# Layer 0's squares summed on TensorE, the plain products of the seven moved in front, and the last output projection by seven products too

## The chip, the cores and the metric

One NeuronCore of one Trainium2 chip runs the whole kernel in one launch. The metric is the device time of that launch in microseconds (us), the median of several runs. Where a sum is made against one profiled execution, that execution's own time and span are used.

## The reference, cut to what matters

A decoder trunk of two layers on 512 tokens of 1024 channels, all in float32. In each layer:

```
hdn = rms_norm(x, norm_w)                     # x: 512 x 1024
u   = hdn @ w_in                              # w_in: 1024 x 10240
q,k,v,z of branch A; q,k,v,z of branch B; gates ga, gb = split(u)
ya  = dilated_mixture(qa, ka, va) * silu(za)  # 16 heads of 64
yb  = rms_norm(diff_attention(qb, kb, vb)) * silu(zb)   # 8 heads of 128
merged = sigmoid(ga) * (ya @ w_proj_a) + sigmoid(gb) * (yb @ w_proj_b)
x   = x + merged @ w_out
```

and after both layers `out = rms_norm(x, final_norm_w)`. A rotation of part of q and k by tables of cosines and sines, the causal masks and the scalar lambda of the second branch do not bear on this change.

## The kernel before, in words

**Operands.** Activations lie with the channels on the partitions: eight blocks m of 128 channels x 512 tokens. Every float32 operand of a large product is split in two fp32r parts, a rounded one (`hi`, a ScalarE copy) and the rest (`lo`, a VectorE subtraction), and a product is three matmuls: hi.hi, hi.lo, lo.hi. `h_block` (L186) makes the two parts of one block of x times norm_w; the factor 1/rms of each token is applied later, to the results.

**Weights** come in the order in which `plan` (L917) lists them, in pieces of 128 x 1024 that `load_to` loads on SyncE's queue (L96), and `split` makes `whi` on ScalarE (L102) and `wlo` on VectorE (L103), into pools of three buffers each. `prep_to(i)` is called from the steps of a projection and keeps this two pieces ahead.

**Two ways to project.** `proj_T` (L270) takes 256 output channels by 512 tokens: 16 steps of three 128x512 matmuls into a PSUM tile `pj` of pool `psj` (three buffers). The first one of a layer (`first=True`, the silu gate z0) goes block by block over k, into two tiles of pool `pss` (tag "s"), and calls `rstd_cols` and `layer_tables` at its end. `proj_V` (L307) is for the last output projection alone: 256 channels at a time, four times, for each of four token blocks eight steps of three 128x256 matmuls, into `pv`. `proj_S` (L329) is for v: tokens and contraction are halved, the 1024 output channels come in two halves, and the product is made of seven quarter products in place of eight, in a scheme after Strassen and Winograd. Product i is 8 steps (kk = 0 to 3, a = 0, 1) of three 128x512 matmuls. Products 0, 3 and 6 take plain blocks of h; 1, 2, 4 and 5 take sums S1 to S4 of h's quarters, which `h_sums` makes on VectorE (L221 to L227) and `h_split` splits (L234, L235). The weight quarters 11, 21, 22 are plain; T1 = 12 - 11 and T3 = 12 - 22 are made by `sum_of` (L108): a ScalarE copy times -1 (L111), then a DMA of the POOL queue that adds 12 to it from memory (L112); T2 = T1 - 22 and the last "21" + T2 are VectorE's (L134, L136). Products go to X (pool `pss`, two buffers), Y (`psj`) and Z (pool `pst`, two buffers); `keep` copies a partial result on ScalarE (L349), `add` joins two on VectorE (L353).

**The front.** For layer 0 the blocks of x arrive by DMA (L801, L804). ScalarE makes each block's h (L188), its squares (`sq_block`, L202) and later x times norm_w in place (`h_full`, L197); VectorE the lo part (L189). GpSimd adds the first seven squares one to the other (L206). `rstd_cols` (L242) sums over channels by eight float32 matmuls with a column of ones (L248): two tiles of squares by four token blocks; VectorE adds the two halves (L250, L251), GpSimd raises to the power -1/2 (L240). `rstd_rows` and `layer_tables` spread the result over the partitions (`rb`), and `ev_z` multiplies a gate's PSUM tile by it (L461). Layer 1 does the same with blocks that layer 0's output projection makes one by one.

**The order** within a layer: z0, z1, v of branch A, one q-k projection, v of branch B, then all other projections with the attention heads merged between them, then `pb` (four projections of yb) and the output projection. A scheduler orders each engine's queue by data and program order, and gives out the buffers; the pool `blk` has 29 buffers of 4 KB a partition, which hold h, the operand parts, the raw quarters of weights, y, the gates, `mg` (the merged operand) and, at the end, `xo` (residual, four) and `fwb` (final norm weight, one).

**The end.** `pb`'s evacuation (L716 to L725) makes a block of merged (L720, L721) and splits it to `mg` (L724, L725). `final_out` (L764) adds each 128 x 256 result to the residual (L770), takes squares with a running sum (L772, ScalarE), multiplies by the final norm's weight (L778); after the fourth piece of a token block come the sum and factor (L775 to L777), two scalings (L780 on ScalarE, L782 on VectorE) and two output DMAs (L781, L783).

Of the kernel before, what the change touches and what calls it, by code (L numbers as in the profile page):

```python
# [16 lines left out]
P = 128  # L17
# [6 lines left out]
BIG = 1e30  # L24
SWAP = [(i ^ 8) if i < 16 else i for i in range(32)]
# [7 lines left out]
def trunk_kernel(ctx: ExitStack, tc: tile.TileContext, x, ws, norm_w, subln_w, final_w, lams, negb, rope, ident_in,  # L33
# [148 lines left out]
    st_ = {"y": {}, "z": {}, "v": {}, "qk": {}}  # L182
# [16 lines left out]
    def sq_block(m, xt):  # L199
# [3 lines left out]
        if m == 0:  # L203
# [38 lines left out]
    def rstd_cols():  # L242

        ps = pst.tile([P, T], F32, tag="t", name="ps_ss")
        for n, sq in enumerate((st_["acc"], st_["sq7"])):
            for tb in range(4):
                c = 4 * n + tb
                nc.tensor.matmul(ps[:, c:c + 1], sq[:, tb * P:(tb + 1) * P], ones[:, 0:1], start=True, stop=True)  # L248
        r = small.tile([P, 4], F32, tag="rstd", name="rstd", bufs=2)
        nc.vector.tensor_copy(r, ps[:, 0:4])  # L250
        nc.vector.tensor_tensor(r, r, ps[:, 4:8], OP.add)  # L251
        inv_sqrt(r, r, 1.0 / D, 1e-6)
# [15 lines left out]
    def proj_T(what, rhs, evac, first=False):  # L268
# [38 lines left out]
    def proj_V(what, lhs, evac):  # L307

        steps = []
        c, j0 = next_chunk(what)  # L310
        hold = {}

        def step(tb, k):
            if tb == 0 and k == 0:
                prep_to(j0 + 2)
            if k == 0:
                hold[tb] = psj.tile([P, T], F32, tag="pj", name=f"pv{c}_{tb}")
            hb, t = lhs(k), slice(tb * P, tb * P + P)
            tok3(hold[tb][:, :256], hb[:, 0, t], hb[:, 1, t], j0 + k // 4, 256 * (k % 4), 256, k == 0, k == 7)
            if tb == 3 and k == 3:  # L320
                prep_to(j0 + 3)
            if k == 7:
                evac(tb, hold.pop(tb))
        for tb in range(4):
            for k in range(8):
                steps.append((360, lambda tb=tb, k=k: step(tb, k)))
        return steps

    def proj_S(what, evac, hook=None):  # L329
# [385 lines left out]
    def pb(layer, i):  # L715

        def ev(b, ps):
# [93 lines left out]
    with tc.manual_schedule(engines={mybir.EngineType.Activation, mybir.EngineType.DVE}):  # L811
        for m in range(NB):
# [8 lines left out]
            if m > 1:  # L821
                sq_block(m - 2, xs[m // 2 - 1][:, m % 2])
# [187 lines left out]
```

## Time and profile before

| | us |
|---|---|
| median of 3 runs | 1391.7 |
| lowest, highest | 1388.79, 1391.72 |
| the profiled execution | 1392.57 |
| its span in the trace | 1390.8 |

The trace gives every instruction's start and length on TensorE (PE; its weight loads PEld), VectorE (DVE), ScalarE (ACT), GpSimd (POOL) and SyncE (SP; a q behind an engine's name is its queue). Times are from the start of the span. Matmuls are pipelined: a 128x512 matmul has a length of 0.39 us, and the next one starts before it ends. PEclk is the granted TensorE clock as a share of 2.4 GHz.

### The profile page before, as it was taken

Reading aid. Unit: us, or ns where it says so; the run is one execution under the profiler, and the core shown is the slowest. Engines: PE = TensorE matmul, PEld = TensorE weight load, DVE = VectorE, ACT = ScalarE, POOL = GpSimd, SP = SyncE. Lnnn points to the kernel's source line nnn. Section 1 sums busy time; section 2 is a strip of 40 time slices with the busy share of each in tenths; the row PEclk is TensorE's granted clock in tenths of the full one; section 3 lists DMA queues with packets and bytes.
Section 4 is the critical chain, followed back from the end, with each engine's and each line's share of the span. In section 5 each row is a group of like instructions: output and inputs, shape, how many; then the busy total and the mean of one; then the engine's idle time right before and its main releaser. Section 6 shows DMA issues by size and latency. Waiting matters only on the chain.

```text
span 1390.8 us, 19560 instructions
## 1 busy us (share of the span) xinstructions
PE 1356.6 (98%) x6728; PEld 1138.8 (82%) x6728; DVE 971.6 (70%) x1900; ACT 859.2 (62%) x1630; POOL 335.7 (24%) x459
## 2 busy tenths in 40 slices
PE   7999999999999999999999999999999999999996
PEld 5788887878888888888878888877888888888896
DVE  6766887779767786545576777797796678664553
ACT  8655678877565757523566566778756566664332
POOL 4120342334303241110220224232350133211000
PEclk9999999999999999999999999999999999999998
DMA  9663574546735564433686366554565364535321
GB/s 305 172 165 123 131 188 102 164 129 158 177 121 144 136 175 116 127 107 91 201 252 150 96 177 159 145 139 121 145 171 163 110 186 114 152 95 162 115 91 61
DMA packets 82019, 202.95 MB, mean 146 GB/s; under 512 B 11136, under 2 KB 27648, under 8 KB 81920
## 3 DMA queue, kind: packets, MB, share of 16 engines
q1 hardware_dynamic: 45312, 134.57, 31.0%
q0 software_dynamic: 19712, 58.74, 18.8%
q10 hardware_dynamic: 16896, 8.39, 2.1%
q8 instruction: 53, 0.87, 0.3%
q14 instruction: 46, 0.38, 0.1%
HBM read 134.55 MB, written 16.78 MB: 109 GB/s over the span
## 4 chain that ended last, share of the span: by engine, by line
PE 91%; DVE 3%; DMA 2%; ACT 1%; issue 1%; POOL 1%; SPq 0%; POOLq 0%; DVEq 0%; ACTq 0%
PE pj L282 21%; PE pj L283 21%; PE pj L284 21%; PE X L304 2%; PE X L305 2%; PE X L303 2%; PE Y L304 1%; PE Y L305 1%; PE Y L303 1%; PE pv L303 1%; PE pv L305 1%; PE pv L304 1%; DMA T<-ws_d 1%; DMA kx(1, 0, 2)0_7658<-hl(1, 0, 2)1_7655 1%; DVE wlo L103 1%
## 5 line engine op out<-in xcount | busy, mean ns | idle before, releaser
L282 PE MATMUL pj<-h,whi 128*128 128x512 f32 x1024 | 405.4, 397 | 7.6 <-DVE whi L817 6.5
L283 PE MATMUL pj<-h,whi 128*128 128x512 f32 x1024 | 407.0, 397 | 1.2 <-DVE h L189 1.1
L284 PE MATMUL pj<-h,wlo 128*128 128x512 f32 x1024 | 403.5, 396 | 0.0
L103 DVE TENSOR_TENSOR wlo<-raw,whi 128x1024 fp32r<-128x1024 f32 x207 | 264.8, 1280 | 103.8 <-ACT whi L102 103.3
L102 ACT ACTIVATE whi<-raw 128x1024 fp32r<-128x1024 f32 x207 | 219.0, 1059 | 148.1 <-PE pj L283 95.5
L282 PEld LDWEIGHTS pj<-h,whi 128*128 128x128 f32 x1024 | 193.4, 189 | 47.0 <-issue 6.5
L283 PEld LDWEIGHTS pj<-h,whi 128*128 128x128 f32 x1024 | 193.6, 189 | 39.3 <-DVE h L189 2.9
L284 PEld LDWEIGHTS pj<-h,wlo 128*128 128x128 f32 x1024 | 193.6, 189 | 37.1 <-DVE wlo L103 0.3
L712 POOL TENSOR_TENSOR g<-g,pr 128x512 f32<-128x512 f32 x16 | 21.0, 1313 | 151.4 <-ACT g L711 126.4
L206 POOL TENSOR_TENSOR sq<-sq,sq 128x512 f32<-128x512 f32 x12 | 19.7, 1642 | 88.1 <-ACT sq L202 87.7
L103 DVE TENSOR_TENSOR wlo<-T,whi 128x1024 fp32r<-128x1024 f32 x24 | 29.3, 1224 | 15.2 <-ACT whi L102 15.1
L304 PE MATMUL pv<-wlo,mg 128*128 128x256 f32 x128 | 35.7, 283 | 0.0
L305 PE MATMUL pv<-whi,mg 128*128 128x256 f32 x128 | 35.7, 283 | 0.0
L303 PE MATMUL pv<-whi,mg 128*128 128x256 f32 x128 | 35.4, 283 | 0.0
L720 DVE TENSOR_TENSOR g<-pj,g 128x512 f32<-128x512 f32 x16 | 11.1, 692 | 30.5 <-PE pj L284 30.5
L102 ACT ACTIVATE whi<-T 128x1024 fp32r<-128x1024 f32 x24 | 25.2, 1056 | 10.8 <-DVE T L134 3.9
L709 DVE TENSOR_TENSOR g<-pj,rb 128x512 f32<-128x512 f32 x32 | 21.4, 686 | 10.8 <-PE pj L284 10.6
L724 ACT ACTIVATE mg<-g 128x512 fp32r<-128x512 f32 x16 | 10.1, 632 | 29.5 <-DVE g L721 29.5
L112 POOL DMA_DIRECT2D T<-ws_d x16 | 14.6, 930 | 53.9 <-ACT T L111 43.3
L303 PE MATMUL X<-whi,h 128*128 128x512 f32 x64 | 23.9, 402 | 3.7 <-DVE z(0, 0, 0)_292 L461 2.5
L496 ACT ACT_TABLE_LOAD x21 | 26.9, 1283 | 0.4
L304 PE MATMUL X<-wlo,h 128*128 128x512 f32 x64 | 25.8, 403 | 0.4 <-DVE wlo L103 0.4
(4000 smaller groups left out, 3307.6 us busy)
## 6 DMA issues: line engine op xcount, KB each, us to landing
raw<-ws_d SPq DMA_DIRECT2D x199, 512.0 KB, 3.9
T<-ws_d POOLq DMA_DIRECT2D x16, 512.0 KB, 7.8
v_dram<-c ACTq DMA_DIRECT2D x24, 256.0 KB, 2.6
pa_dram<-pa SPq DMA_DIRECT2D x16, 256.0 KB, 3.0
pr<-pa_dram SPq DMA_DIRECT2D x16, 256.0 KB, 4.1
v_dram<-v ACTq DMA_DIRECT2D x8, 256.0 KB, 5.9
xr<-x_d SPq DMA_DIRECT2D x8, 256.0 KB, 4.5
x_dram<-xr SPq DMA_DIRECT2D x8, 256.0 KB, 2.7
```

Of the source, the lines that this page charges most:

```text
L102: nc.scalar.activation(whi[j], src, AF.Copy)
L103: nc.vector.tensor_tensor(wlo[j], src, bits(whi[j]), OP.subtract)
L206: nc.gpsimd.tensor_tensor(st_["acc"], st_["acc"], s, OP.add)
L282: nc.tensor.matmul(ps, w_h, hb[:, 0], start=(k == 0), stop=False)
L283: nc.tensor.matmul(ps, w_h, hb[:, 1], start=False, stop=False)
L284: nc.tensor.matmul(ps, w_l, hb[:, 0], start=False, stop=(k == 7))
L303: nc.tensor.matmul(ps, hh, w_h, start=first, stop=False, skip_group_check=True)
L304: nc.tensor.matmul(ps, hh, w_l, start=False, stop=False, skip_group_check=True)
L305: nc.tensor.matmul(ps, hl, w_h, start=False, stop=last, skip_group_check=True)
L496: nc.scalar.activation(p, p, AF.Exp, bias=mn[:, i:i + 1], scale=-1.0, accum_out=den[:, i:i + 1])
L709: nc.vector.tensor_tensor(g[:, b], ps, rb, OP.mult)
L712: nc.gpsimd.tensor_tensor(g[:, 0], g[:, 0], st_.pop(("pa", m)), OP.mult)
```

## The change

Three parts. **First**, layer 0's squares are no longer added on GpSimd: `sq_block` sums each block over its channels at once by four float32 matmuls with the column of ones, into one PSUM tile of pool `pst` that is cleared first and read by `inv_sqrt` directly. x times norm_w for layer 0 is made by VectorE in place of ScalarE. Layer 1 keeps GpSimd's additions. **Second**, the seven products run in the order 0, 3, 1, 2, 4, 5, 6, the two that need plain h and plain weights first; loads, weight splits and sums are reordered to match, the first tile of z0 goes to pool `pso` and its second to `psj`, so that X's pool `pss` is free, and product 6 runs a = 0 before a = 1. S3 and S4 are computed together with S1 and S2. **Third**, the last output projection is made by `proj_S` in place of `proj_V`: merged is kept in float32 too (`mf`, four buffers of `blk`), S1 to S4 are made of it, and the evacuation works on 128 x 512.

```diff
+ORDER = (0, 3, 1, 2, 4, 5, 6)
...
-            need += [n + k for k in (3, 4, 4, 4, 5, 6, 6, 6)] + [n + 8] * 6
+            need += [n + 3, n + 4, n + 5, n + 6] + [n + 6] * 4 + [n + 8] * 6
...
-        if i < 2:
-            q[c, "22", p] = raw.pop(l0 + 2 + p)
-        elif i in (6, 7):
-            q[c, "21", p] = raw.pop(l0 + 4 + p)
-        name = ("11", "T1", "T2", "21", "T3", "22", "21")[i // 2]
+        if i in (2, 3):
+            q[c, "21", p] = raw.pop(l0 + 2 + p)
+            q[c, "22", p] = raw.pop(l0 + 4 + p)
+        name = ("11", "21", "T1", "T2", "T3", "22", "21")[i // 2]
         split(j, flat(q[c, name, p]))
-        if i < 2:
+        if i in (2, 3):
             sum_of(c, "T3", p, q[c, "22", p], ws[l0 + 6 + p])
-        elif i < 4:
+        elif i in (4, 5):
...
-    def sq_block(m, xt):
+    def sq_block(layer, m, xt):
         s = t2(f"sq{m}")
         nc.scalar.activation(s, xt, AF.Square)
-        if m == 0:
+        if layer == 0:
+            if m == 0:
+                st_["ps_ss"] = pst.tile([P, T], F32, tag="t", name="ps_s0")
+                nc.vector.memset(st_["ps_ss"][:, 0:4], 0.0)
+            for tb in range(4):
+                nc.tensor.matmul(st_["ps_ss"][:, tb:tb + 1], s[:, tb * P:(tb + 1) * P], ones[:, 0:1], start=False,
+                                 stop=(m == 7), skip_group_check=True)
+        elif m == 0:
             st_["acc"] = s
...
+        if "ps_ss" in st_:
+            inv_sqrt(r, st_.pop("ps_ss"), 1.0 / D, 1e-6)
+        else:
...
-                pool, tag = (pss, "s") if first else (psj, "pj")
+                pool, tag = (pso, "o") if first and b == 0 else (psj, "pj")
...
-        for i in range(7):
-            for kk in range(4):
-                for a in range(2):
-                    steps.append((683, lambda i=i, kk=kk, a=a: step(i, kk, a)))
+        for i in ORDER:
+            for kk, a in [(kk, a) for kk in range(4) for a in range(2)] if i != 6 else [(kk, a) for a in range(2) for kk in range(4)]:
+                steps.append((683, lambda i=i, kk=kk, a=a: step(i, kk, a)))
...
-            nc.vector.tensor_tensor(g[:, 0], g[:, 0], g[:, 1], OP.add)
+            f = g[:, 0]
+            if layer + 1 == DEPTH:
+                hf = st_["hf"].setdefault(DEPTH, {})
+                if b == 0:
+                    hf[i] = f4(f"mf{i}")
+                f = hf[i][:, b]
+            nc.vector.tensor_tensor(f, g[:, 0], g[:, 1], OP.add)
...
-    def final_out(i):
+    def final_out():
+        seen = set()
-        def ev(tb, ps):
+        def ev(tb, n, src):
+            r = xo[tb][:, n]
+            nc.vector.tensor_tensor(r, src, r, OP.add)
+            scr = t2(f"scr{n}{tb}")
+            nc.scalar.activation(scr, r, AF.Square, accum_out=ssq[:, tb, n:n + 1])
+            both = tb in seen
+            seen.add(tb)
+            if both:
                 rs = small.tile([P, 2], F32, tag="rf", name=f"rf{tb}")
-                nc.vector.tensor_reduce(rs[:, 0:1], ssq[:, tb], mybir.AxisListType.X, OP.add)
+                nc.vector.tensor_tensor(rs[:, 0:1], ssq[:, tb, 0:1], ssq[:, tb, 1:2], OP.add)
...
-            nc.vector.tensor_tensor(r, r, f, OP.mult)
+            nc.vector.tensor_tensor(r, r, fwb[:, n], OP.mult)
...
-        return lambda: proj_V((DEPTH - 1, "out", i), lambda k: st_["mg", k], ev)
+        return proj_S((DEPTH - 1, "out"), ev)
...
     for m in range(NB):
-        h_full(0, m, xs[m // 2][:, m % 2])
+        xt = xs[m // 2][:, m % 2]
+        nc.vector.tensor_scalar(xt, xt, nw[:, 0, m:m + 1], None, OP.mult)
...
-            run(chain(*[final_out(i) for i in range(4)]))
+            f = final_out()
+            h_sums(DEPTH, ("S1", "S2"))
+            h_split(DEPTH, ("S1", "S2"))
+            h_sums(DEPTH, ("S3", "S4"))
+            run(f[:12] + [(0, lambda: h_split(DEPTH, ("S3", "S4")))] + f[12:])
```

## Rows read from the trace of the kernel before

**Rows 1.** The page's first two parts: busy time of TensorE over the span, and the mean busy share of the 16 DMA engines in 40 slices of the span (tenths).
```profile
PE 1356.6 (98%) x6728; PEld 1138.8 (82%) x6728; DVE 971.6 (70%) x1900; ACT 859.2 (62%) x1630; POOL 335.7 (24%) x459
...
DMA  9663574546735564433686366554565364535321
```

**Rows 2.** Busy time by stretch (us from the span's start): length, then busy time and count of PE, PEld, DVE, ACT, POOL, then granted clock, DMA share, GB/s.
```profile
38.00:46.00 8.00, 5.51 (x16) 4.16 (x17) 8.00 (x16) 2.68 (x3) 0.00 (x0) 0.79 1.02 303
41.90:45.40 3.50, 3.50 (x10) 2.71 (x9) 3.50 (x8) 0.73 (x1) 0.00 (x0) 0.51 1.03 335
46.00:84.00 38.00, 38.00 (x170) 31.43 (x169) 25.28 (x32) 27.31 (x34) 2.63 (x3) 1.00 0.54 129
287.70:291.10 3.40, 3.40 (x9) 2.47 (x10) 3.40 (x10) 0.75 (x4) 2.56 (x2) 0.50 0.74 239
...
1311.00:1333.00 22.00, 22.00 (x106) 18.18 (x105) 11.75 (x15) 8.01 (x12) 0.00 (x0) 1.00 0.26 89
1346.00:1380.00 34.00, 33.98 (x284) 33.77 (x282) 16.25 (x38) 11.81 (x31) 1.64 (x3) 1.00 0.19 63
```

**Rows 3.** What PE waited for in the first 60 us, after the first load: us in total, times, longest.
```profile
PE X L303 <- DVE z(0, 0, 0)_292 L461: 2.5, 1, 2.5
PE ps_ss L248 <- POOL sq L206: 1.2, 1, 1.2
...
PE Y L303 <- ACT whi L102: 0.9, 1, 0.9
```

**Rows 4.** The timeline of layer 0's front on PE: start, length, engine, line, operation, count, and the idle time before it.
```profile
14.04 0.39 PE L284 MATMUL pj<-h,wlo 128*128 128x512 f32 x1
...
24.43 1.95 PE L248 MATMUL ps_ss<-ones,sq 128*128 128x1 f32 x16 [1.22 <-POOL sq L206]
26.24 0.48 PE L284 MATMUL pj<-h,wlo 128*128 128x512 f32 x1
...
36.69 0.39 PE L284 MATMUL pj<-h,wlo 128*128 128x512 f32 x1
...
40.99 0.50 PE L303 MATMUL X<-whi,h 128*128 128x512 f32 x1 [2.49 <-DVE z(0, 0, 0)_292 L461]
...
48.17 0.39 PE L303 MATMUL Y<-whi,S 128*128 128x512 f32 x1
```

**Rows 5.** The timeline on PE where layer 1 passes from z1 to v.
```profile
717.85 0.39 PE L284 MATMUL pj<-h,wlo 128*128 128x512 f32 x1
719.47 0.50 PE L303 MATMUL X<-whi,h 128*128 128x512 f32 x1 [1.23 <-DVE z(1, 0, 0)_6533 L461]
...
723.37 0.50 PE L304 MATMUL X<-wlo,h 128*128 128x512 f32 x1 [0.40 <-DVE wlo L103]
```

**Rows 6.** The chain of work that ended last, in v's stage of layer 0: start, length, what. The rows are the first matmuls of two products that follow one another.
```profile
58.99 0.45 PE Z L303 x2
...
64.43 0.45 PE X L303 x2
```

**Rows 7.** The timeline of the last output projection: its first and last matmul on PE, then the last token block's evacuation on DVE, ACT, DVE and ACT.
```profile
1333.74 0.28 PE L303 MATMUL pv<-whi,mg 128*128 128x256 f32 x1
...
1379.70 0.28 PE L305 MATMUL pv<-whi,mg 128*128 128x256 f32 x1
...
1380.01 0.42 DVE L770 TENSOR_TENSOR xo<-pv,xo 128x256 f32<-128x256 f32 x1
...
1380.53 0.42 ACT L772 ACTIVATE scr<-xo 128x256 f32<-128x256 f32 x1 [0.37 <-DVE xo L770]
...
1381.15 0.41 DVE L778 TENSOR_TENSOR xo<-xo,fwb 128x256 f32<-128x256 f32 x1
...
1382.29 0.72 ACT L780 ACTIVATE xo<-xo,rf 128x512 f32<-128x512 f32 x1 [1.24 <-POOL rf L777]
```

**Rows 8.** The timeline of layer 0's front on DVE, POOL and ACT; the second and third row merge four and six instructions.
```profile
10.31 0.75 DVE L189 SCALAR_TENSOR_TENSOR h<-x,nw,h 128x512 fp32r<-128x512 f32 x1 [1.10 <-ACT h L188]
...
14.15 6.88 DVE L189 SCALAR_TENSOR_TENSOR h<-x,nw,h 128x512 fp32r<-128x512 f32 x4
...
13.57 10.81 POOL L206 TENSOR_TENSOR sq<-sq,sq 128x512 f32<-128x512 f32 x6 [12.52 <-ACT sq L202]
...
18.04 1.66 ACT L202 ACTIVATE sq<-x 128x512 f32<-128x512 f32 x3
```

**Rows 9.** DVE's groups by line and shape: busy time, mean ns of one, idle time before. Then, from DVE's timeline, instructions that follow one another without a gap, in pairs or single.
```profile
L721 DVE TENSOR_TENSOR g<-g 128x512 f32<-128x512 f32 x16 | 11.1, 693 | 0.8
...
L782 DVE TENSOR_SCALAR xo<-xo,rf 128x512 f32<-128x512 f32 x4 | 1.9, 488 | 2.3 <-POOL rf L777 2.3
...
28.57 1.28 DVE L225 TENSOR_TENSOR S3f<-x 128x512 f32<-128x512 f32 x2
29.77 1.29 DVE L227 TENSOR_TENSOR S4f<-x,S2f 128x512 f32<-128x512 f32 x2
...
57.14 1.22 DVE L136 TENSOR_TENSOR raw<-raw,T 128x1024 f32<-128x1024 f32 x1
58.28 1.22 DVE L103 TENSOR_TENSOR wlo<-raw,whi 128x1024 fp32r<-128x1024 f32 x1
```

**Rows 10.** DMA issues of the weights: size of one, median us from issue to landing.
```profile
raw<-ws_d SPq DMA_DIRECT2D x199, 512.0 KB, 3.9
T<-ws_d POOLq DMA_DIRECT2D x16, 512.0 KB, 7.8
```

More of the change, by code (lines that the diff above doesn't have):

```diff
@@ L180, in trunk_kernel @@
     nc.gpsimd.memset(bits(pt1[:, :, 0:128]), 0.0)
-    st_ = {"y": {}, "z": {}, "v": {}, "qk": {}}
+    st_ = {"y": {}, "z": {}, "qk": {}, "mg": {}}
     def h_block(layer, m, xt):
@@ L242, in rstd_cols @@
     def rstd_cols():
[L244 to L248, printed above, removed]
-        r = small.tile([P, 4], F32, tag="rstd", name="rstd", bufs=2)
-        nc.vector.tensor_copy(r, ps[:, 0:4])
-        nc.vector.tensor_tensor(r, r, ps[:, 4:8], OP.add)
-        inv_sqrt(r, r, 1.0 / D, 1e-6)
+        r = small.tile([P, 4], F32, tag="rstd", name="rstd", bufs=2)
+        if "ps_ss" in st_:
+            inv_sqrt(r, st_.pop("ps_ss"), 1.0 / D, 1e-6)
+        else:
+            ps = pst.tile([P, T], F32, tag="t", name="ps_ss")
+            for n, sq in enumerate((st_["acc"], st_["sq7"])):
+                for tb in range(4):
+                    c = 4 * n + tb
+                    nc.tensor.matmul(ps[:, c:c + 1], sq[:, tb * P:(tb + 1) * P], ones[:, 0:1], start=True, stop=True)
+            nc.vector.tensor_copy(r, ps[:, 0:4])
+            nc.vector.tensor_tensor(r, r, ps[:, 4:8], OP.add)
+            inv_sqrt(r, r, 1.0 / D, 1e-6)
         st_["rcol"] = r
@@ L305, in tok3, with proj_S @@
         nc.tensor.matmul(ps, hl, w_h, start=False, stop=last, skip_group_check=True)
[L307 to L329, printed above, removed]
+    def proj_S(what, evac):
         steps = []
@@ L335, in proj_S @@
         X, Y, Z, cp = {}, {}, {}, {}
+        plain = st_["mg"] if what[1] == "out" else st_["h"]
         def operand(i, kk, a):
             if i in (0, 3, 6):
-                hb = st_["h"][kk + (0, 4)[i > 0]]
+                hb = plain[kk + (0, 4)[i > 0]]
                 o = 128 * a + (256 if i == 6 else 0)
@@ L372, in step @@
         def step(i, kk, a):
-            if a == 0 and kk % 2 == 0:
-                prep_to(j0 + 2 * i + kk // 2 + 2)
+            if kk % 2 == 0:
+                prep_to(j0 + 2 * ORDER.index(i) + kk // 2 + 2)
             if kk == 0:
@@ L741, in ev @@
             nc.sync.dma_start(x1_dram[layer, m], r)
-            sq_block(m, r)
+            sq_block(layer + 1, m, r)
             h_full(layer + 1, m, r)
-        return lambda: [(0, pre)] + proj_T((layer, "out", i), lambda k: st_["mg", k], ev)
+        return lambda: [(0, pre)] + proj_T((layer, "out", i), lambda k: st_["mg"][k], ev)
     xo = {}
@@ L858, in trunk_kernel @@
         z0, z1 = zz(layer, 0, 0, True)(), zz(layer, 0, 1)()
-        run(z0 + z1[:4] + [(0, lambda: h_sums(layer, ("S1", "S2"))), (0, lambda: h_split(layer, ("S1", "S2")))] + z1[4:])
+        run(z0 + z1[:4] + [(0, lambda: h_sums(layer, ("S1", "S2"))), (0, lambda: h_split(layer, ("S1", "S2"))),
+                           (0, lambda: h_sums(layer, ("S3", "S4")))] + z1[4:])
+        v = vs(layer, 0)()
+        run(v[:12] + [(0, lambda: h_split(layer, ("S3", "S4")))] + v[12:])
         if layer == 0:
             lambdas()
-        v = vs(layer, 0)()
-        run(v[:4] + [(0, lambda: h_sums(layer, ("S3", "S4")))] + v[4:12] + [(0, lambda: h_split(layer, ("S3", "S4")))] + v[12:])
         run(qk(layer, 0, 0)())
@@ L884, in trunk_kernel @@
             nc.sync.dma_start(fwb, bass.AP(tensor=final_w.tensor, offset=final_w.offset, ap=[[0, P], [1, D]]))
-            ssq = small.tile([P, 4, 4], F32, tag="ssq", name="ssq", bufs=1)
+            ssq = small.tile([P, 4, 2], F32, tag="ssq", name="ssq", bufs=1)
             run(chain(*[pb(layer, i) for i in range(4)]), residual_cols(0) + residual_cols(1))
-            run(chain(*[final_out(i) for i in range(4)]))
+            f = final_out()
[3 more added lines that the diff above has]
+            run(f[:12] + [(0, lambda: h_split(DEPTH, ("S3", "S4")))] + f[12:])
         else:
@@ L924, in plan @@
         order = [("z", 0, 0), ("z", 0, 1), ("v", 0), ("qk", 0, 0), ("v", 1)] + [n for p in PARTS for n in p[0]]
-        order += [(n, i) for n in ("pb", "out") for i in range(4)]
+        order += [("pb", i) for i in range(4)] + ([("out", i) for i in range(4)] if layer + 1 < DEPTH else [("out",)])
         for n in order:
-            kind = "S" if n[0] == "v" else "T"
+            kind = "S" if n[0] == "v" or n == ("out",) else "T"
             chunks.append((kind, (layer, *n)))
```

29 lines of the change are left out of this document (10 added, 19 removed).

## The prediction

> **What bounds the kernel now.** I read the page's busy times first: TensorE is busy 98% of the span, so time is won only by taking matmul time out or by filling holes between matmuls [rows 1]. Next the stretches. In the whole stage of seven products PE has no hole (38.00 of 38.00 us) and DVE is busy 25 of 38; in the last output projection PE has none either (33.98 of 34.00) while DVE is busy 16 of 34; the hole lies at 38 to 46, PE 5.5 us busy of 8 [rows 2]. The waits name it: X's first matmul waits 2.5 us for z0's evacuation, because z0 holds pool `pss`; 0.9 us go to a weight half, 1.2 us to GpSimd's sum of squares [rows 3]. Behind it the clock is granted at 0.51 from 41.9 to 45.4, its 1.2 GHz level: that is 1.7 us of work lost, after PE had run one matmul between 36.9 and 41.0 [rows 2, 3, 4]. Layer 1 has the same wait, 1.23 us, and one of 0.40 [rows 5].
>
> **The price of a matmul.** Two products of v start 5.44 us apart [rows 6]; that is 24 matmuls of 512 columns, 0.227 us each. The last projection's 384 matmuls of 256 columns run from 1333.74 to 1379.70 [rows 7]: 45.96 / 383 = 0.120 us each. So a column costs 0.000443 us in the wide ones and 0.00047 in the narrow.
>
> **Part 1, the front of layer 0.** Eight square tiles x 4 matmuls with ones make 64 instructions on PE where 16 stood (each call appears as two): 16 took 24.43 to 26.24, 0.113 us each [rows 4], so 64 cost 7.2 us, 5.4 more. They stay on PE's path, since PE is behind its data from here on. In return GpSimd's six additions (10.8 us) go. While they run, DVE's lo parts take 1.7 us each (four in 6.88), against 0.75 before [rows 8], and PE waits for them: so h's last four blocks come by ScalarE's pace. ScalarE also sheds the eight copies of `h_full`; DVE gets eight tensor_scalars, 0.49 each by the nearest row (L782) [rows 9], 3.9 us. I put these at nothing: z1's eleven us of matmuls cover them; without cover they would cost 3.9.
> New path: at 14.27 PE has done blocks 0 to 3 of z0 [rows 4]. What is left until product 0 is done: 24 matmuls of z0, 48 of z1, 24 of product 0, 96 x 0.227 = 21.8; squares 7.2; the four transposes for rb 0.5. If it never waits it ends at 43.8. The last squares are out at 19.7 even now [rows 8], when PE still has 3 us of z0 queued. Before, product 0 ended at 48.17, with one stray matmul of Y in it: 47.9. Gain 4.1.
> No wait for z0 is left: product 0 goes to X in `pss`, now free, product 3 to Z in `pst`; Y, which needs a `psj` buffer of z0 or z1, starts 10.9 us later. No hole, so no fall of the clock, I take.
> Bounds: the squares' matmuls can each hold up PE's in-order queue for ScalarE, and if the clock falls once that is another 1.7 us; that gives 1.0. If GpSimd's release lets h come still earlier, and weight loads hide under matmuls, 5.5.
> The Trainium skill (TensorE: Matmul & The Clock Gate, Back-to-back issue gap) gives a matmul of up to 64 columns about 25 ns. By that figure the squares would cost an estimated 1.6 us and this part's gain be 9.7. The trace has 113 ns, with a 128*128 weight tile for each, and decides.
>
> **Part 2, the new order elsewhere.** In layer 1 the two holes go: 1.23 + 0.40 = 1.6 us. Bounds 0 (another wait takes their place) and 2. After product 0 PE never waited in layer 0 (46 to 84 us) [rows 2]; I take the other stages of v to be alike, so there the order changes nothing. T1 moves from third to fifth place among the splits, which slackens its adding DMA (7.8 us to land against 3.9 for a plain load) [rows 10]; weight quarter 21 is needed 5.4 us after the start in place of 16. Its load is 3.9 us and is issued ahead: nothing, unless `blk` has no buffer (below). Queues: T3's two adds leave POOL later, and GpSimd's queue is emptier than before.
>
> **Part 3, the last projection.** PE: 7 x 5.44 = 38.1 us in place of 46.1: 8.0 less. But DVE, half idle there, gets the sums. Counted from the stage's start to PE's last matmul: 13 lo parts of weights, 2 T2 and 2 sums "21"+T2, 17 of 128x1024; three operations of the last `mg`; 4 sums S that need the last blocks (the other 4 fit into the idle 10 of 22 us of `pb` [rows 2]); 6 of 8 lo parts of S; 6 joins; 7 residual adds and 7 norm products: 33 of 128x512; 3 scalings. One behind the other, 128x1024 takes 1.14 us (57.14 to 58.28), 128x512 0.60 (two in 1.20) [rows 9]. Sum 19.4 + 19.8 + 1.5 = **40.7 us**, above PE's 38.1. With each at its full length, 1.22 and 0.69, it is 45.0. So the end is no longer TensorE's alone.
> I measure to the last block's scaling, at 1382.29, 48.55 us after the start [rows 7]; what follows (two DMAs and the end) stays. PE bound: 38.1, then the present 2.47 from the last matmul to the scaling, and 0.75 for a block twice as wide (add 0.42 to 0.69, square 0.42 to some 0.62, as three in 1.66, product 0.41 to 0.69 [rows 7, 8, 9]): 41.3, a gain of 7.2. DVE bound: 40.7, then of the last block's 3.2 us (2.47 + 0.75) what queued work cannot fill: its add and product, 1.2, and two waits on ScalarE and GpSimd, an estimated 0.55 each; 43.0, a gain of 5.5. At full lengths 47.3, a gain of 1.2. I take 43.0, since the count is nearer to back-to-back. DVE's lag delays first the residual adds and norm products, which nobody waits for until the end; if the scheduler puts them ahead of weight parts, PE waits in their place, and the sum is the same.
> Buffers: at the start of the stage `blk` holds 8 y (freed one by one in the last 5 us of `pb`), 8 mg, 4 mf, 4 xo, fwb, 2 quarters 11, 2 T1: 29 of 29. Quarters 21 and 22 get the y's places 5 us ahead, and land 3.9 us later. So I put buffers at nothing, with no room to spare.
> The Trainium skill (same page and section) puts the spacing at N/2.4 + 2.5 ns, 216 and 109 ns here. By it PE's part would shrink from 41.9 to 36.3, by 5.6 and not 8.0. This trace has 227 and 120, and decides.
>
> **Sum.** 4.1 + 1.6 + 5.5 = 11.2 us from the profiled execution's 1392.6: 1381.4. That execution stands 0.9 above the median of the runs, so against the median it is 1380.5. I say **1381**.
>
> **The rivals.**
> *The last stage gives little.* DVE's work at full lengths, or PE waiting for lo parts behind evacuations, leaves 1.2 us: 1392.6 - 4.1 - 1.6 - 1.2 - 0.9 = 1384.8 against the median. For it: 40.7 against 38.1 has no slack. Against: much of it can slide past PE's end. 0.2.
> *The front's gain is not there.* The wait for z0 was only the last of several: the DMA engines' share is 1.02 from 38 to 46 us [rows 2], so quarter 21, now wanted at 44, could come late, or the squares' 5.4 us eat the rest. Then part 1 gives 0 and the time is 1392.6 - 1.6 - 5.5 - 0.9 = 1384.6. For it: that share. Against: quarter 21's competitors, 22 and T3, move behind it. 0.13.
> *Slower: `blk` runs dry in the last stage.* If 21 and 22 get buffers only as mg's first four go, 5.4 us into the stage, then product 3 waits for load (3.9) and split (2.2): 6 us, and a clock fall of 1.7. The same at T3 and T2, three times in all: 23 us, against 5.5 + 5.7 gained: 1380.5 + 23 = 1403. It decides when more than 11 us are lost, that is from the second such wait on. For it: the count of 29. Against: y's eight places come free before. 0.05.
> *The change does not do what it says*, the scheduler ordering PE as before: 1391 to 1392. 0.04.
>
> **How the numbers follow.** Forecast 0.58; rivals 0.2, 0.13, 0.05, 0.04. The ends of the three terms, 1.0 + 0 + 1.2 and 5.5 + 2 + 7.2, give 1389.5 and 1377.0 against the median; a clock fall as at 287.7 [rows 2], 1.7 us, may come or go with the shift. All lowest ends at once is unlikely; both middle rivals lie near 1385, with 1.7 us for a clock fall near 1387; one more fall less than today takes the low end to 1375.5. Range **1375.5 to 1387**. Over 0.2% (2.8 us, about what a measurement of this kernel can tell from no change) faster: forecast, two middle rivals, less a share where two of these meet, 0.87; within 0.06; slower 0.07.
>
> **What would show each step.** Front: product 0's last matmul at about 44, PE's idle time before X gone, 64 ps_ss instructions of 0.11 us, DVE's lo parts at 0.75 with no GpSimd additions beside them, clock 1.0 from 42 to 45. Layer 1: no wait between z1 and X. End: from the first X matmul to PE's last 38 to 40 us, DVE busy over 90% in that stretch, the last scaling 43 us after the start. I am wrong if PE waits in the last stage for DMA or for VectorE by more than 3 us, if product 0 still ends past 47, or if holes arise in branch A's v stage.

## The result, and the profile after

The changed kernel takes 1404.82 us (median of 6 runs, 1402.84 to 1407.73) where the kernel before takes 1391.71 (6 runs, 1388.79 to 1392.28): 1.0103 of the time, 95% interval 1.0091 to 1.0114. The forecast was 1381, a gain of 11 us; it became a loss of 13. The profiled execution is the fastest of the six, 1402.84 us with a span of 1401.1.

The page first (it answers to [rows 1]): matmul records went from 6728 to 6560, and TensorE's busy time rose all the same, by 6 us.

```profile
PE 1362.8 (97%) x6560; PEld 1137.4 (81%) x6560; DVE 992.1 (71%) x1923; ACT 867.0 (62%) x1630; POOL 329.8 (24%) x457
...
DMA  9636574545735454332576456554565373535431
...
raw<-ws_d SPq DMA_DIRECT2D x197, 512.0 KB, 3.8
T<-ws_d POOLq DMA_DIRECT2D x20, 512.0 KB, 7.5
```

Busy time by stretch, columns as in [rows 2]. The hole at 38 to 46 is gone, as forecast. In its place stands a stretch of 13.65 us at half clock, in which PE is busy from end to end. Half clock comes four times more, for 3.4 us each; the last row is the last projection from its first matmul to its last:

```profile
14.81:28.46 13.65, 13.65 (x59) 12.97 (x59) 13.10 (x26) 9.19 (x14) 2.99 (x3) 0.51 1.05 369
38.00:46.00 8.00, 8.00 (x37) 6.62 (x36) 5.69 (x6) 3.44 (x4) 3.13 (x2) 1.00 0.59 143
46.00:84.00 38.00, 37.99 (x168) 31.14 (x167) 23.21 (x22) 24.84 (x31) 1.74 (x2) 1.00 0.50 127
294.80:298.20 3.40, 3.40 (x9) 2.62 (x9) 3.40 (x10) 1.97 (x6) 1.88 (x2) 0.51 0.44 171
799.90:803.30 3.40, 3.40 (x10) 2.60 (x9) 1.22 (x1) 0.61 (x1) 0.00 (x0) 0.52 0.02 7
977.50:980.90 3.40, 3.40 (x10) 2.65 (x9) 3.25 (x7) 2.09 (x6) 1.64 (x2) 0.50 0.61 202
1363.20:1366.60 3.40, 3.40 (x10) 2.63 (x9) 3.40 (x5) 0.72 (x2) 0.00 (x0) 0.50 0.00 0
1343.20:1388.20 45.00, 40.66 (x169) 32.26 (x167) 41.84 (x59) 26.58 (x42) 3.25 (x4) 0.96 0.13 24
```

PE's timeline in the front (compare [rows 4]). 56 of the 64 one-column matmuls stand in one block ahead of z0's later blocks. X follows z1 with no wait, and product 0's last matmul starts at 50.25:

```profile
12.76 0.95 PE L208 MATMUL ps_s<-ones,sq 128*128 128x1 f32 x8
...
14.12 11.18 PE L208 MATMUL ps_s<-ones,sq 128*128 128x1 f32 x56
25.16 0.77 PE L292 MATMUL pj<-h,whi 128*128 128x512 f32 x1
...
44.81 0.39 PE L294 MATMUL pj<-h,wlo 128*128 128x512 f32 x1
45.03 0.39 PE L313 MATMUL X<-whi,h 128*128 128x512 f32 x1
...
50.25 0.39 PE L315 MATMUL X<-whi,h 128*128 128x512 f32 x1
```

What PE waited for, in three stretches (0 to 130, 690 to 810, 1335 to 1395; us in total, times, longest). The waits of [rows 3, 5] for z0's evacuation and for GpSimd's squares are gone. Three new kinds have come: 2.0 us in each stage of branch B's v, 1.5 us behind layer 1's z1, 4.3 us in the last stage:

```profile
PE X L313 <- ACT c L338: 2.0, 1, 2.0
...
PE X L313 <- ACT c L338: 2.0, 1, 2.0
PE X L314 <- DVE wlo L104: 1.5, 1, 1.5
...
PE Y L314 <- DVE wlo L104: 4.3, 2, 2.9
```

The last stage's first and last matmul and its last scalings (compare [rows 7]): 44.7 us of matmuls where 46.0 were, and 3.75 us from the last matmul to the last scaling where 2.59 were.

```profile
1343.21 0.39 PE L313 MATMUL X<-whi,mg 128*128 128x512 f32 x1
...
1387.93 0.39 PE L315 MATMUL X<-whi,mg 128*128 128x512 f32 x1
...
1391.68 1.04 DVE L777 TENSOR_SCALAR xo<-xo,rf 128x512 f32<-128x512 f32 x2 [0.37 <-POOL rf L772]
1391.68 1.33 ACT L775 ACTIVATE xo<-xo,rf 128x512 f32<-128x512 f32 x2 [1.35 <-POOL rf L772]
```

**Where the 10.3 us between the two profiled spans (1390.8 and 1401.1) arose**, by PE's milestones: branch A's v of layer 0 ends 2.8 us later; branch B's v adds 2.3; the rest of layer 0 adds 0.9; layer 1's front and branch A's v give 0.1 back (the wait for z0 is gone, one for a lo part has come); layer 1's branch B and the way to the last stage add 3.5; the last stage gives 1.2 back; the tail behind PE's last matmul takes 2.1 more.

Counted by the clock, the kernel before has three stretches of half clock while PE works, the two of [rows 2] and this one:

```profile
966.90:970.30 3.40, 3.24 (x8) 2.46 (x9) 3.40 (x10) 0.99 (x5) 2.26 (x2) 0.50 0.89 236
```

Each costs 1.7 us of work, 5.1 together; in the changed kernel one of 13.65 and four of 3.4 us cost 13.6. So some 8.5 of the 10.3 us are lost at half clock: 5.1 more in the front, 1.7 each behind the waits that end at 799 and 1362. Such a stretch comes or goes with the execution: near 285 to 295 PE waits some 2 us in all in every kernel traced, and half clock follows in the kernel before and the changed one but not in e6, e8, e9 and e10 below. A difference of 1.7 us between two profiled executions therefore proves little by itself.

### The profile page after: what moved, and what is told of

Read it like the earlier page. It is cut to its first block, busy times and chain, and to the rows that moved or that the text cites. A ratio compares the mean times of both kernels' runs of the same rounds, so it can differ in the third digit from the quotient of the medians.

```text
span 1401.1 us, 19220 instructions
## 1 busy us (share of the span) xinstructions
PE 1362.8 (97%) x6560; PEld 1137.4 (81%) x6560; DVE 992.1 (71%) x1923; ACT 867.0 (62%) x1630; POOL 329.8 (24%) x457
## 4 chain that ended last, share of the span: by engine, by line
PE 88%; DVE 5%; DMA 3%; ACT 1%; issue 1%; POOL 1%; SPq 0%; ACTq 0%; DVEq 0%; POOLq 0%
PE pj L292 21%; PE pj L293 21%; PE pj L294 21%; PE X L313 2%; PE X L314 2%; PE X L315 2%; DMA T<-ws_d 1%; DVE wlo L104 1%; DMA raw<-ws_d 1%; PE Y L314 1%; PE Y L315 1%; PE ps_s L208 1%; PE Y L313 1%; DVE S L242 0%; DMA x<-x_d 0%
## 5 line engine op out<-in xcount | busy, mean ns | idle before, releaser
L104 DVE TENSOR_TENSOR wlo<-T,whi 128x1024 fp32r<-128x1024 f32 x30 | 36.6, 1221 | 21.5 <-ACT whi L103 21.5
L113 POOL DMA_DIRECT2D T<-ws_d x20 | 18.1, 949 | 129.6 <-ACT T L112 114.9
L103 ACT ACTIVATE whi<-T 128x1024 fp32r<-128x1024 f32 x30 | 31.7, 1056 | 16.9 <-DMA T<-ws_d 8.3
L314 PE MATMUL Y<-wlo,S 128*128 128x512 f32 x80 | 32.0, 399 | 4.3 <-DVE wlo L104 4.3
L313 PE MATMUL X<-whi,S 128*128 128x512 f32 x80 | 30.7, 404 | 4.0 <-ACT c L338 4.0
L314 PE MATMUL X<-wlo,S 128*128 128x512 f32 x80 | 32.0, 400 | 0.0
L315 PE MATMUL Y<-whi,S 128*128 128x512 f32 x80 | 31.9, 398 | 0.0
L315 PE MATMUL X<-whi,S 128*128 128x512 f32 x80 | 31.8, 397 | 0.0
L112 ACT ACTIVATE T<-raw 128x1024 f32<-128x1024 f32 x20 | 20.5, 1052 | 15.2 <-DMA raw<-ws_d 10.9
L313 PE MATMUL Y<-whi,S 128*128 128x512 f32 x80 | 28.4, 395 | 0.0
```

Source lines behind the costliest of these rows:

```text
L103: nc.scalar.activation(whi[j], src, AF.Copy)
L104: nc.vector.tensor_tensor(wlo[j], src, bits(whi[j]), OP.subtract)
L112: nc.scalar.activation(flat(t), flat(of), AF.Copy, scale=-1.0)
L313: nc.tensor.matmul(ps, hh, w_h, start=first, stop=False, skip_group_check=True)
L314: nc.tensor.matmul(ps, hh, w_l, start=False, stop=False, skip_group_check=True)
L315: nc.tensor.matmul(ps, hl, w_h, start=False, stop=last, skip_group_check=True)
```

## The experiments

Twelve kernels ran. Ratios are to the kernel before, run on the same chip in the same session. A name stands for the kernel from here on. The kernel before measured 1390.75 to 1391.71 in these sessions, so medians of two sessions compare to about 1 us.

| kernel | squares of layer 0 | T3 | last projection | median us | ratio (95%) |
|---|---|---|---|---|---|
| changed | TensorE, in a block | late | seven products | 1404.82 | 1.0103 (1.0091 to 1.0114) |
| e1 | GpSimd | late | seven products | 1399.99 | 1.0072 (1.0058 to 1.0085) |
| e2 | TensorE, in a block | early | seven products | 1392.60 | 1.0014 (1.0006 to 1.0023) |
| e3 | TensorE, in a block | late | as before | 1400.14 | 1.0066 (1.0052 to 1.0079) |
| e4 | TensorE, spread | late | seven products | 1399.10 | 1.0064 (1.0050 to 1.0077) |
| e5 | TensorE, in a block | early | no lo parts | 1387.10 | 0.9972 (0.9961 to 0.9983) |
| e6 | TensorE, spread | early | as before | 1387.92 | 0.9976 (0.9966 to 0.9986) |
| e7 | TensorE, spread | early | sums in other places | 1386.32 | 0.9961 (0.9948 to 0.9973) |
| e8 | TensorE, spread | early | and T2 by DMA | 1385.97 | 0.9959 (0.9946 to 0.9973) |
| e9 | GpSimd | early | as before | 1391.44 | 0.9998 (0.9988 to 1.0009) |
| e10 | TensorE, spread | issue late | as before | 1393.03 | 1.0019 (1.0007 to 1.0031) |
| e11 | TensorE, spread | early | seven products | 1389.29 | 0.9988 (0.9977 to 0.9998) |
| e12 | TensorE, spread | late | as before | 1396.56 | 1.0036 (1.0023 to 1.0049) |

**e1: layer 0's squares back on GpSimd.**

```
-        if layer == 0:
...
-        elif m == 0:
+        if m == 0:
             st_["acc"] = s
```

> Layer 0's squares go back to GpSimd's six additions and 16 one-column matmuls; all else is as changed. Theory: the block of 56 one-column matmuls (14.1 to 25.2 us at 0.197 us each, half clock) costs the front its gain; without it z1 ends near 41 as before, X starts at once, branch A's products are done 3 to 5 us earlier than 83.4, and the time is 1398 to 1400 against 1403 for the changed kernel's profiled execution. Rival: the new order of products costs it (another weight quarter second); then branch A's products still end at 82 to 84 and the time stays at 1402 to 1404.

Measured 1399.99: X starts at 39.91 and product 0's last matmul at 46.49, 3.8 us earlier than in the changed kernel. The block of squares costs some 5 us of the median; the order does not cost it here. The profiled execution of e1 has half clock too in its front, from 17.9 to 24.7 us, behind a wait of 1.9 us for h.

**e4: the same 64 matmuls, each square's behind a later block of z0.**

```
+SQ_AT = (2, 3, 4, 5, 6, 7, 7, 7)
...
+            if first and b == 1 and st_["sqs"]:
+                for m in range(8):
+                    if SQ_AT[m] == k:
+                        sq_ones(m)
```

> The same 64 one-column matmuls, but each square's stand behind a later block of z0 (blocks 2 to 7) in place of ahead of z0; all else as changed. Theory: it is their standing together ahead of real work, with the clock falling meanwhile, that costs: spread out they take 0.113 us each at full clock, product 0 ends 3 to 5 us earlier than 50.5, the time is 1398 to 1400. Rival: 64 one-column instructions cost 11 us wherever they stand and the clock falls all the same: product 0 ends at 49 to 51, the time is 1401 to 1404.

Measured 1399.10; product 0's last matmul starts at 46.22. So it is where they stand that counts. Windows of e6, which has the same front, show it: PE is busy through 14 to 26 us, as in the changed kernel, but at full clock.

```profile
14.00:26.00 12.00, 12.00 (x78) 10.72 (x77) 12.00 (x24) 12.00 (x18) 2.88 (x3) 1.00 1.04 395
24.00:36.00 12.00, 11.80 (x67) 9.98 (x66) 11.27 (x17) 5.44 (x9) 5.22 (x2) 1.00 1.06 285
```

But only five squares stand in groups of eight matmuls; `SQ_AT` puts the last three in one row of 24 (2.73 us in e6, from 25.01). Of the seven traced kernels with this front, e6, e8 and e10 keep full clock through it; e4, e7 and e11 fall to half for 3.4 us right behind the row, e12 for 6.8 us from its end on. Behind a group of eight none fell. No run splits that row, so that it causes the fall is argued from its place. In e4:

```profile
28.20:31.60 3.40, 3.40 (x9) 2.65 (x9) 3.40 (x5) 1.06 (x1) 0.88 (x2) 0.50 1.06 274
```

**e2: quarter 22 loaded ahead of 21 again, T3's copy and adding DMA issued at the stage's first two splits.**

```
-        if i in (2, 3):
-            q[c, "21", p] = raw.pop(l0 + 2 + p)
-            q[c, "22", p] = raw.pop(l0 + 4 + p)
+        if i < 2:
+            q[c, "22", p] = raw.pop(l0 + 2 + p)
+        elif i in (2, 3):
+            q[c, "21", p] = raw.pop(l0 + 4 + p)
...
-        if i in (2, 3):
+        if i < 2:
             sum_of(c, "T3", p, q[c, "22", p], ws[l0 + 6 + p])
```

> The quarter 22 is loaded ahead of 21 again and T3's copy and adding DMA are issued at the stage's first two splits, as before the change; the order of the products stays as changed. Theory: T3's adding DMA, now issued behind the moves of the last query/key head on GpSimd's queue, is what PE waits for in both stages of branch B's v (2.03 and 1.99 us, and a clock fall of 1.7 us in layer 1); the waits go and the time falls by 4 to 6 us, to 1397 to 1399. Rival: a quarter that now lands later, or a buffer that T3 holds longer, puts another wait in the place: within 1.5 us of the changed kernel, 1401 to 1404.

Measured 1392.60: the largest single cost, 12.2 us, more than twice what was expected. The waits in branch B's v of both layers and the one behind layer 1's z1 are gone. GpSimd's timeline in the changed kernel, branch B's v of layer 0: the two adding DMAs of T3 are issued from 106.20 on, behind the moves of the last head's keys, which wait for their evacuation.

```profile
96.45 1.32 POOL L394 TENSOR_TENSOR sw(0, 0, 0)1_806<-sw(0, 0, 0)1_806,st 128x512 f32<-128x512 f32 x1
102.30 0.54 POOL L386 DMA_DIRECT2D kx(0, 0, 0)0_815<-hl(0, 0, 0)1_812  x1 [4.53 <-ACT hl(0, 0, 0)1_812 L401]
...
104.68 1.53 POOL L386 DMA_DIRECT2D kx(0, 0, 0)1_819<-hl(0, 0, 0)1_812  x3
106.20 1.85 POOL L113 DMA_DIRECT2D T<-ws_d  x2
```

ScalarE's timeline: it comes to the splits of T3 some 5 us after the issue and waits 2.34 and 1.84 us for the landing. The copy of product 2 out of X, which PE waits for at 118.25, has nothing to do with T3; it stands behind the second split on ScalarE's queue. The first row shows the two copies that the adding DMAs need: they end at 104.7 and 105.7, so the moves of the keys hold the issues up by some 1.5 us only. The rest of the lateness is the copies' own place, two splits later in the order: in e2 they start at 64.04 and 92.70.

```profile
103.67 2.00 ACT L112 ACTIVATE T<-raw 128x1024 f32<-128x1024 f32 x2
...
113.76 1.06 ACT L103 ACTIVATE whi<-T 128x1024 fp32r<-128x1024 f32 x1 [2.34 <-DMA T<-ws_d]
116.66 1.06 ACT L103 ACTIVATE whi<-T 128x1024 fp32r<-128x1024 f32 x1 [1.84 <-DMA T<-ws_d]
117.62 1.07 ACT L338 ACTIVATE c<-X 128x512 f32<-128x512 f32 x2
```

The Trainium skill (TensorE: Matmul & The Clock Gate, Architectural detail) calls the queues of ScalarE and VectorE strictly first in, first out; these rows agree. In e2 the two are issued at 65.38 and 95.22, the second one between the moves of queries and of keys:

```profile
65.38 0.87 POOL L113 DMA_DIRECT2D T<-ws_d  x1 [1.37 <-ACT T L112]
...
95.22 0.97 POOL L113 DMA_DIRECT2D T<-ws_d  x1
```

**e10 and e12: the late issue alone, then with the order of the loads.** e10 is e6 with `if i < 2` ahead of T3's `sum_of` turned back to `if i in (2, 3)`; e12 is e6 with all of the changed kernel's handling of T3.

> As the run with T3 early, squares spread and the last projection as before (1387.9), but T3's copy and adding DMA are issued at the splits of quarter 21 again; the loads keep their order, 22 ahead of 21. Theory: the lateness of that issue alone is the cost: PE waits some 2 us in each stage of branch B's v again, the time is 1395 to 1400. Rival: the order of the loads was the cost, or the buffers that it holds: 1387 to 1390.

> The changed kernel with the squares spread and the last projection as before the change: all of T3's handling is the change's, so it differs from the run with T3's issue alone late (1393.0) in the order of the loads alone (21 ahead of 22), and from the run with neither (1387.9) in both. Theory: the order of the loads costs more, by the wait for a lo part behind z1 in layer 1 (1.0 to 1.5 us in every kernel that has it, in none without): 1394.5 to 1397. Rival: only the late issue costs, and the rest of T3's 12 us came from the clump and the last stage: 1392 to 1394.

Measured 1393.03 and 1396.56, against 1387.92: by the medians the late issue costs 5.1 us (the time 2 us under the range expected), the order of the loads 3.5 more, within the theory's range; but the intervals of the two ratios overlap. In e10 PE waits 3.8 and 2.3 us in the two stages of branch B's v, each followed by a stretch at half clock (in layer 0, 104.4 to 121, granted 0.90 against 1.00 in e6). The order of the loads acts in layer 1's front. There 22's two loads are issued among several others, after 21's, and land 12.1 and 15.7 us after their issue. ScalarE stands before T3's copy until it is there: rows of e12, then of e10, where 22 goes first.

```profile
711.48 1.06 ACT L113 ACTIVATE T<-raw 128x1024 f32<-128x1024 f32 x1 [5.75 <-DMA raw<-ws_d]
...
716.26 1.06 ACT L113 ACTIVATE T<-raw 128x1024 f32<-128x1024 f32 x1 [2.78 <-DMA raw<-ws_d]
```

```profile
705.81 1.06 ACT L113 ACTIVATE T<-raw 128x1024 f32<-128x1024 f32 x1 [1.39 <-DMA raw<-ws_d]
```

Behind those copies stand the splits of S3 and S4, `rb` and the next weights, and PE ends up waiting 1.0 us for a lo part and 0.6 for the rstd rows in e12, for neither in e10. So 1.6 us of the order's price are seen. In layer 0's branch B e12 waits 1.5 us less than e10, and PE's waits from 7 us on come to about 15 us in both. The profiled spans differ by 4.5 us, but e12 loses 10.2 us at half clock and e10 3.4. Whether the order costs more than 1.6 us is open.

**e9: the new order without the squares and the seven products at the end**, that is e2 with e1's squares and e3's last projection.

> The new order of the products with T3 early, the squares on GpSimd, the last projection as before the change: part 2 alone, with X no longer waiting for z0. Against it the run with the squares spread on TensorE (1387.9) differs in the squares alone. Theory: squares that stand between z0's blocks on TensorE are worth 1 to 3 us, since GpSimd's additions no longer slow VectorE's lo parts: 1389 to 1391. Rival: the squares are worth nothing where they stand and all of the gain is the order's: 1387 to 1388.5.

Measured 1391.44, ratio 0.9998. That is not the order alone, though: x times norm_w stays on VectorE, as changed. There its operations stand between the lo parts of h and take 1.51 us each beside GpSimd's additions (0.48 in e6, without them), so that the lo parts start 3.1 us apart, where before the change four took 6.88 [rows 8]. PE waits 4.8 us for h, and 1.1 before. VectorE's timeline in e9:

```profile
15.06 1.75 DVE L190 SCALAR_TENSOR_TENSOR h<-x,nw,h 128x512 fp32r<-128x512 f32 x1
16.74 1.51 DVE L831 TENSOR_SCALAR x<-x,nw 128x512 f32<-128x512 f32 x1
18.17 1.76 DVE L190 SCALAR_TENSOR_TENSOR h<-x,nw,h 128x512 fp32r<-128x512 f32 x1
```

So the order, X's freedom from z0 and this move are together worth nothing that can be measured; no run has the order without the move. Against e9, e6 has only the squares on TensorE, spread, and is 3.5 us faster, a little more than expected: GpSimd's additions gone, PE no longer waits 4.8 us for h in the front.

**e6: parts 1 and 2 without the two costs.**

> T3 early, squares spread behind z0's blocks, last projection as before the change: parts 1 and 2 alone, without the two costs found. Theory: the gains of the front and of the new order add: 4 us less than T3 early for the squares, 1 less for the last stage, 1386 to 1388.5. Rival: a gain of the front is given back in a later stage that waits for weights: 1390 to 1392.5.

Measured 1387.92, as expected.

**e3, e11: the last stage.** e3 is the changed kernel with the 384 matmuls of 256 columns and their evacuations back; e11 is e6 with the seven products.

> The last output projection goes back to 384 matmuls of 256 columns with their evacuations; squares and order stay as changed. Theory: the last stage's seven products give nothing, because VectorE sets their pace (PE 45.0 us against 46.1, and 2.0 us more from PE's last matmul to the end): the time changes by less than 2 us, 1401 to 1404. Rival: the last stage did gain several us and the loss ahead of it was larger than the milestones say: the time rises by 4 us or more, 1407 or later.

> T3 early, squares spread, and the last projection by seven products as the change has it. Against the run with the old last projection (1387.9) it differs in part 3 alone. Theory: with VectorE's queue in the order of the change, PE's stage is 44.8 us and the tail behind it 13 against 11.4, so part 3 costs 0 to 2 us: 1388 to 1390. Rival: with the other two costs gone it gains what was forecast, 1382 to 1384.

e3 went against the theory's size: it is 4.7 us faster by the medians, though its profiled span, 1399.2, is only 1.9 shorter. e11 is the cleaner comparison: 1389.29 against 1387.92, 1.4 us, though the intervals of the ratios overlap. The traces tell it more closely: from the stage's first matmul to the end of the span it takes 57.1 us in every kernel with the old projection (before, e3, e6, e9, e10, e12) and 57.7 to 58.0 in the five with the new one as written (changed, e1, e2, e4, e11). So part 3 as written costs 0.7 to 0.9 us. Half clock behind PE's wait of 2.9 us takes 1.7 us in each of the five; without it the part would gain an estimated 0.9.

**e5: the last stage without the lo parts of its weights.**

```
+        if j >= first_prep[-1]:
+            wlo[j] = whi[j]
+            return
```

> As the run with T3 early (1392.6), but in the last output projection alone the 14 lo parts of the weights are not computed (the hi part is used in their place: this leaves out 14 operations of 128x1024 on VectorE, some 16 us; PE's matmuls, loads, sums and buffers of the weights stay). Theory: VectorE's queue sets the pace of that stage; without this work PE's stage falls from 44.8 us to 38 to 40 and the time to 1384 to 1387.5. Rival: the quarters come late for want of buffers (29 of 29) or through the adding DMAs; then PE still waits 3 us or more there and the time is 1390 to 1393.

Measured 1387.10, 5.5 us less than e2. PE's stage falls from 44.8 to 38.7 us, all but 0.5 of its waits gone. Loads, adding DMAs and buffers were as in e2, so `blk` with its 29 of 29 was not what PE waited for. The stretches of e11 and of e5, first matmul to last:

```profile
1330.40:1375.20 44.80, 40.41 (x168) 32.26 (x167) 41.55 (x59) 24.52 (x40) 2.08 (x3) 0.96 0.13 22
```

```profile
1338.90:1377.60 38.70, 38.15 (x169) 31.27 (x167) 28.52 (x46) 24.87 (x41) 2.43 (x3) 1.00 0.15 26
```

**e7: the same work of VectorE in another order; e8: four sums less for it.**

```
+            g[1].insert(2, (0, lambda: h_sums(DEPTH, ("S3",), (0,))))
+            g[2].insert(2, (0, lambda: h_sums(DEPTH, ("S3",), (1,))))
+            g[3].insert(2, (0, lambda: h_sums(DEPTH, ("S1", "S2", "S4"), (0,))))
...
+            for at, name in ((23, "S4"), (17, "S3"), (9, "S2"), (3, "S1")):
+                f.insert(at, (0, lambda name=name: (h_sums(DEPTH, (name,)), h_split(DEPTH, (name,)))))
```

```
+                sum_of(c, "T2", p, q[c, "22", p], flat(q[c, "T1", p]))
...
+            nc.gpsimd.dma_start(out=flat(q[c, "21", p]), in_=flat(q[c, "T2", p]), accum_op=OP.add)
```

> T3 early, squares spread, seven products last; there the sums S3 and the first halves of S1, S2, S4 are emitted inside the stage before, and each sum's split just ahead of its product, in place of all ahead of the first. Theory: it is the order of VectorE's queue that makes PE wait for lo parts (1.4 and 2.9 us), not the sum of its work: PE's stage falls from 44.8 to 39 to 41 us, the time to 1382 to 1385. Rival: the sum of VectorE's work (about 41 us) sets the end whatever its order: PE's stage stays above 42.5, the time 1386.5 to 1389.

> As the run with the sums' order changed, and in the last stage T2 and 21+T2 are made by ScalarE copies and adding DMAs, which takes 4 operations of 128x1024 (4.6 us) from VectorE. Theory of the sum: each us taken from VectorE comes off the end, 3 to 4.6 us less than the run with the order changed. Theory of the order: at most 1.5 us less. Rival: the adding DMAs land later than VectorE's sums would be done, and PE waits for T2: 1 us or more slower than it.

e7 measured 1386.32, 3.0 less than e11, and PE's stage is 41.3 us, 0.3 above the range given; the time is 1.3 above the theory's range and 0.2 below the rival's. From the stage's first matmul to the end of the span it takes 54.5 us, 3.5 less than e11. VectorE's work in the stage falls by 2.0 us (39.5 against 41.55), since some of the sums now come before it; at least the other 1.5 us are the order's. PE still waits 2.6 us. The tail did not shrink (3.75 us from the last matmul to the last scaling, as in the changed kernel).

```profile
1329.80:1371.10 41.30, 38.71 (x169) 31.08 (x167) 39.52 (x55) 23.91 (x40) 1.26 (x2) 1.00 0.13 27
```

e8 measured 1385.97, within 1.5 us of e7, as the theory of the order says; four sums off VectorE (35.5 us busy against 39.5) bring the stage 0.4 us. But it does not part the theories cleanly, since ScalarE waits there for the adding DMA of T2, which e7 has not:

```profile
1345.55 1.06 ACT L104 ACTIVATE whi<-T 128x1024 fp32r<-128x1024 f32 x1 [4.58 <-DMA T<-T]
```

The changed kernel's VectorE timeline shows the order at fault. PE waits until 1362.52 for the lo part that starts at 1361.26; ahead of it stand splits of S3, whose product comes two places later, a T2 and a sum on 21 for later products, and two evacuations:

```profile
1356.59 0.68 DVE L342 TENSOR_TENSOR c<-Z,c 128x512 f32<-128x512 f32 x1
1357.19 0.68 DVE L242 TENSOR_TENSOR S<-S3f,S 128x512 fp32r<-128x512 f32 x1
1357.79 1.21 DVE L134 TENSOR_TENSOR T<-T,raw 128x1024 f32<-128x1024 f32 x1
1358.92 0.68 DVE L242 TENSOR_TENSOR S<-S3f,S 128x512 fp32r<-128x512 f32 x1
1359.52 0.68 DVE L342 TENSOR_TENSOR c<-Z,c 128x512 f32<-128x512 f32 x1
1360.12 1.21 DVE L136 TENSOR_TENSOR raw<-raw,T 128x1024 f32<-128x1024 f32 x1
1361.26 1.21 DVE L104 TENSOR_TENSOR wlo<-T,whi 128x1024 fp32r<-128x1024 f32 x1
```

**The sum, and what stays open.** From e6 (1387.92): T3's handling 8.6 (e12), part 3 1.4 (e11), the block of squares 3.3 (e2 less e11) make 1401.2. The changed kernel's profiled execution took 1402.84, its median is 1404.82, so 3.6 us of the median belong to none of the three alone (T3's handling gave 12.2 there, in e2). One candidate shows in e5, which has the same block: in its profiled execution, the slowest of its ten, the clock was still granted at half between 30 and 34 us, and X started at 49.54 where the changed kernel's trace has 45.03:

```profile
30.00:34.00 4.00, 4.00 (x11) 3.13 (x10) 1.39 (x2) 2.48 (x4) 0.84 (x1) 0.52 1.06 216
```

How long the clock stays down at the block varies between the traces of kernels that have it: 10.2 us in e2 and e3, 13.65 in the changed kernel, 20.5 in e5. It accounts for the changed kernel's slower executions in part at most: their mean granted clock, 0.986 in the profiled one, is 0.984 in the slowest (1407.73), which is worth about 2.8 us, but 0.986 again at 1405.86 and 1407.52. What makes those slower stays open.

## Why the prediction was wrong

**Part 1, right in size and wrong in place.** Two terms failed. "16 took 24.43 to 26.24, 0.113 us each, so 64 cost 7.2 us": in the trace 8 take 0.81 us and 56 take 11.04, 11.85 together, 4.6 more, because the clock falls to its 1.2 GHz level while they run and a matmul takes 0.197. And "no hole, so no fall of the clock, I take": PE was busy 13.65 of 13.65 us and had waited 0.21 at most. That is also why z0's next eight wide matmuls, 25.16 to 28.68, took 3.5 us in place of 1.8. Together they give 6.3 of the 6.7 us by which product 0 ended late (50.5 against 43.8). The removed wait for z0, X's start behind z1, the cleared clock fall at 42 and the lo parts at 0.75 all came as written. With the squares spread, product 0 ends at 44.9 where it holds the clock (e6), and they are worth 3.5 us against GpSimd's (e9 to e6): the 4.1 of the forecast stood on a mechanism that is there, but the change as scheduled does not use it. "I put these at nothing", of x times norm_w on VectorE, holds only without GpSimd's additions beside it (e9).

**Part 2, the step that failed most.** "Queues: T3's two adds leave POOL later, and GpSimd's queue is emptier than before." The first half was seen and not followed up: T3's copies stood two splits later, its DMA issues behind the moves of the keys besides (some 1.5 us), and T3 was due some 5 us after an issue that takes 7.5 us to land (the page's median for adding DMAs) and here up to 9.8. What was emptier was POOL's compute. "I take the other stages of v to be alike, so there the order changes nothing" is the second error: branch B's v has a query/key head ahead of it, branch A's has none. The third is that quarter 22 got no price at all; only 21 was asked about, and 21 did come in time. A layer's front is where the loads queue up, and there 22's place cost 1.6 us of PE's waits in the trace (3.5 by the medians of e10 and e12). Layer 1's 1.6 us came free and went into those waits; e9, without them, puts the order at nothing together with x times norm_w on VectorE.

**Part 3, the sum right, its use wrong.** VectorE's work was put at 40.7 us and is 41.84 in the stage, which is 45 us long where 38 to 40 were forecast; the last scaling was forecast 43.0 us after the start and came at 48.5, as before the change. The false step is "if the scheduler puts them ahead of weight parts, PE waits in their place, and the sum is the same". It is not: VectorE's later work hangs on PE. A lo part needs the hi part, ScalarE's hi part needs a weight buffer, and that comes free when PE has used it; so when PE is held up early, VectorE runs dry later (3.2 us idle in the 45). VectorE's and then ScalarE's timeline of the changed kernel:

```profile
1377.21 1.23 DVE L104 TENSOR_TENSOR wlo<-raw,whi 128x1024 fp32r<-128x1024 f32 x1 [1.03 <-ACT whi L103]
...
1376.12 1.06 ACT L103 ACTIVATE whi<-raw 128x1024 fp32r<-128x1024 f32 x1 [2.85 <-PE X L315]
```

And the last blocks' chain comes behind PE all the same, 3.75 us in place of 2.3. The rival "the last stage gives little" named the outcome (1.2 us), and "`blk` runs dry", the rival on the slower side, named a place that was innocent (e5). That a late DMA in branch B, or a fall of the clock under busy matmuls, would end on the slower side was no rival at all.

## What to carry to other kernels

When a step moves, write down for each queue on which it issues what it will now stand behind, and for each engine what stands behind the one that waits: here a DMA two splits later stopped ScalarE, and PE waited for a copy that had nothing to do with it. Many tiny matmuls belong between wide ones in small groups, not in a row. And a busy sum that just fits says nothing on its own: it holds only if the engine's order is the order in which the results are due.

## What the runs showed of the hardware

In the changed kernel the granted clock went from 1.00 to 0.51 during a run of 56 one-column matmuls, with PE busy all the time; with 40 of them in groups of eight between wide ones it stayed at 1.00 through 14 to 26 us (e6), and a row of 24 was followed by half clock in four of seven traces. In groups they take 0.101 us each (8 in 0.81), at half clock 0.197. A stretch of half clock behind one and the same wait comes in some traces and not in others. A 512 KB weight load, 3.9 us at the median of e12, landed only 15.7 us after its issue where a layer's front had issued several at once. A VectorE operation of 128x512 with one input tile, 0.48 us alone, took 1.51 us beside GpSimd's additions (e9).
